# Hybrid trunk: output projection as seven block products, longer attention turns, and the first tile's norm weights applied by column

## The chip, the cores and the metric

The kernel runs on one core of a Trainium2 chip. The metric is the device time of one execution in microseconds (us); lower is better. The median of three runs of the kernel before is 843.53 us (843.45 to 843.87). Five engines work side by side, each through its own queue in order: PE (TensorE, matrix products and transposes), DVE (VectorE), ACT (ScalarE), POOL (GpSimd) and SP, whose queue issues nearly all DMAs here. Products are collected in PSUM, operands lie in SBUF, and some intermediate tensors go through DRAM.

## What is computed

One layer on a 1024 x 1024 float32 input (S = D = 1024):

```python
h    = rmsnorm(x, norm_pre)
proj = h @ w_in                      # split by columns
oa   = rmsnorm(diff_attention(qa, ka, va, lam), norm_a) * (1 - lam_init)   # 4 heads, causal, ALiBi
ya   = oa * silu(za)
hb   = rmsnorm(sigmoid(ob) * mlstm(silu(conv(qb)), silu(conv(kb)), vb, ig, fg), norm_b)   # 4 heads
yb   = hb * silu(zb)
merged = sigmoid(ga) * (ya @ w_a) + sigmoid(gb) * (yb @ w_b)
out  = x + rmsnorm(merged @ w_out, norm_post)
```

## The kernel before

Every large product is done with operands cut in two parts, high and low (`split`, L113 to L115: ACT casts the high part, DVE subtracts it for the low part), and three products per block of 128: high x high, high x low, low x high. So a full 128 x 128 x 512 step is three matmuls.

**Opening (L162 to L232, L247, L604 to L627).** `x` comes in eight tiles of 128 tokens. Eight warm-up matmuls on a tile of ones (L168, L169) run first on PE, then two matmuls of one row (L174) spread the row `norm_pre` over 128 partitions, and ACT copies the two halves from PSUM to `npre` (L175). `norm_tile` (L206) squares and sums a tile (L211, L215), takes the power -0.5 on POOL (L221), and multiplies the tile by that factor and by `npre` in one DVE instruction (L223). `turn_tile` (L233) turns the tile by eight PE transposes (L83) and splits the result. `tok_pass` (L292) multiplies it with the first 520 weight columns, in two chunks whose raw parts are `raw_c` and whose split parts are `wc`.

**Seven-product blocks (L316 to L437).** The other projections go by pairs of 128 columns. A pair is a 2 x 2 block product, done with seven products in place of eight (`PRODS`, Winograd's form of Strassen's method). `Combos` forms sums of the blocks of `w_in` on DVE, `Banks` forms the sums of the results: three PSUM banks Y, X, Z, into which products are added, and three copies out (`keep`). One product is 12 matmuls of 512 columns (`product`, L367). The operand of product n+2 is prepared (`prep`) while n runs.

**Weaving (L1011 to L1050).** Products of the projections, and later `merge_b`, are a list of generators, `fill`. Through `weave` the mLSTM and attention chains take from it: after each step of the chain, `weave` emits fill worth a wanted number of us (a step of six matmuls is counted as 1.4), with a debt `left` carried over and at least 0.6 of the wanted share. `attn_head` (L924) does a head in ten turns. Turn i emits `weigh(i-2)` (`pv`), `turn(i-1)` (`pT`), `score(i, 0)` and `score(i, 1)` (`S`, then a DVE reduction L949 and an ACT exponential L956), and `combine(i)` (L965, L966, L970), then yields its share. The transposes `pT` of the next turn need the result of L970. Before the output stage PE's order is pinned to that of the program; the other engines' orders are set by a scheduler.

**The end (L1109 to L1232).** `merge` multiplies `yb` and then `ya` with their weights; each unit (8 x 2 of them) is 12 matmuls, a DVE instruction that applies the gate (L1108) and, for `ya`, the addition of the other branch (L1181) and a split into `M`. The output projection then walks two column halves of `w_out`, eight token tiles each: 24 matmuls into one bank, sum of squares on ACT (L1209), product with `norm_post` on DVE (L1213). In the second half each row is finished: POOL (L1220, L1221), two DVE instructions with `x` (L1226), two stores (L1230).

## Time and profile before

| what | us |
|---|---|
| median of the three runs | 843.53 |
| the profiled execution's own time | 841.9 |
| its span, first to last instruction | 840.2 |
| PE busy | 829.3 (99%) |
| DVE busy | 573.0 (68%) |
| ACT busy | 400.4 (48%) |
| `ya` merge on PE starts | 691.8 |
| output projection on PE starts | 746.3 |

All times below are counted from the span's start. Busy times are unions of intervals. A row such as "2.72 PE ob0Y L80 x12" is twelve matmuls that took 2.72 us together. A bracket at the end of a row, [0.69 <-ACT m L114], is the idle time of the engine before that instruction and what ended it. Names are those of the program's tiles without buffer numbers; a name before the arrow is written, those behind are read. The matmuls' ends are modelled and overlap, so the spacing of starts says more than a single duration.

### The profile page before, as it was taken

The numbers are of one execution on the slowest core, as the hardware profiler recorded it, in microseconds if no ns is written. First come the engines' busy times: TensorE is split into PE (matmuls) and PEld (weight loads), VectorE is DVE, ScalarE is ACT, GpSimd is POOL, SyncE is SP. The second block draws the span as 40 slices with busy tenths as digits, with TensorE's granted clock in tenths as the row PEclk, the third lists the DMA queues.
The fourth block names the chain that finished last, engine by engine and source line by source line (L and its number), as shares of the span: only waits on it lengthen the run. The fifth ranks groups of instructions, "written<-read, shape, count | busy, mean of one in ns | idle before, by whom it ended". The sixth has DMA issues, their size and how long they took to land.

```text
span 840.2 us, 12224 instructions
## 1 busy us (share of the span) xinstructions
PE 829.3 (99%) x4282; PEld 706.5 (84%) x4282; DVE 573.0 (68%) x1161; ACT 400.4 (48%) x892; POOL 36.5 (4%) x70
## 2 busy tenths in 40 slices
PE   9999999999999999999999999999999999999997
PEld 7998888888888888888888888788888888888885
DVE  6996969769659767568767875587587734981133
ACT  6663545444544544446655655466576521341110
POOL 1100000000000000010010000000100000000011
PEclk9999999999999999999999999999999999999999
DMA  7712441451542547266256426442666757830252
GB/s 238 216 40 70 101 151 51 138 163 51 176 143 83 174 146 231 89 208 202 92 161 228 126 74 204 139 162 75 224 208 229 271 184 263 295 105 1 101 200 101
DMA packets 100482, 128.44 MB, mean 153 GB/s; under 512 B 8666, under 2 KB 60098, under 8 KB 100420
## 3 DMA queue, kind: packets, MB, share of 16 engines
q1 hardware_dynamic: 100420, 127.66, 47.9%
q8 instruction: 34, 0.56, 0.3%
q14 instruction: 28, 0.23, 0.1%
HBM read 88.27 MB, written 39.35 MB: 152 GB/s over the span
## 4 chain that ended last, share of the span: by engine, by line
PE 95%; DMA 2%; DVE 1%; ACT 1%; issue 1%; SPq 0%; POOL 0%; DVEq 0%; POOLq 0%; ACTq 0%
PE out L80 10%; PE mrg L80 10%; PE tok L80 6%; PE S L80 4%; PE pv L80 4%; PE pT L83 2%; PE num L80 2%; PE qkb0Y L80 1%; PE g04Y L80 1%; PE g00Y L80 1%; PE za1Y L80 1%; PE g12Y L80 1%; PE g02Y L80 1%; PE zb0Y L80 1%; PE za0Y L80 1%; PE g10Y L80 1%
## 5 line engine op out<-in xcount | busy, mean ns | idle before, releaser
L956 ACT ACTIVATE p<-p,ast 128x128 f32<-128x128 f32 (+7 forms) x64 | 49.5, 775 | 31.2 <-DVE ast L955 23.5
L949 DVE CUSTOM_DVE_ANT_0 p<-S,gm 128x384 f32<-128x384 f32 (+5 forms) x96 | 49.8, 554 | 13.4 <-PE S L80 11.7
L1213 DVE TENSOR_TENSOR o<-out,npost 128x512 f32<-128x512 f32 x16 | 11.1, 691 | 57.3 <-ACT oj L1209 57.3
L80 PE MATMUL mrg<-y,mbw 128*128 128x512 f32 x192 | 44.9, 391 | 0.0
L80 PE MATMUL mrg<-y,maw 128*128 128x512 f32 x192 | 43.7, 389 | 0.0
L1209 ACT ACTIVATE oj<-out 128x512 f32<-128x512 f32 x16 | 9.6, 598 | 71.5 <-PE out L80 71.5
L80 PEld LDWEIGHTS mrg<-y,maw 128*128 128x128 f32 x192 | 36.0, 188 | 7.5
L80 PEld LDWEIGHTS mrg<-y,mbw 128*128 128x128 f32 x192 | 35.8, 188 | 7.3
L80 PEld LDWEIGHTS pv<-va,pT 128*128 128x128 f32 x288 | 37.2, 191 | 2.6
L80 PE MATMUL pv<-va,pT 128*128 128x128 f32 x288 | 37.4, 275 | 0.0
L80 PE MATMUL S<-khh,qs 128*128 128x384 f32 (+5 forms) x96 | 34.9, 369 | 0.3 <-ACT pT L986 0.2
L80 PE MATMUL S<-kll,qs 128*128 128x384 f32 (+5 forms) x96 | 32.4, 342 | 0.4 <-DMA kll<-qk_d 0.4
L1108 DVE SCALAR_TENSOR_TENSOR tg<-tg,mrg 128x512 f32<-128x512 f32 x32 | 21.8, 682 | 14.6 <-PE mrg L80 12.9
L754 DVE SCALAR_TENSOR_TENSOR cv<-pad,cols,cv 128x1024 f32<-128x1024 f32 x24 | 30.7, 1280 | 0.2
L970 DVE SCALAR_TENSOR_TENSOR p<-p,ast,p 128x128 f32<-128x128 f32 (+7 forms) x32 | 26.1, 816 | 0.7
L823 ACT ACTIVATE junk<-raw 128x128 bf16<-128x128 f32 x32 | 9.9, 310 | 31.6 <-DVE raw L818 31.4
L80 PE MATMUL out<-wo,m 128*128 128x512 f32 x96 | 23.7, 395 | 0.0
L83 PE MATMUL pT<-ident,p 128*128 128x128 f32 x144 | 21.2, 274 | 2.5 <-DVE p L970 2.5
L986 ACT COPY pT<-pT 128x512 f32<-128x512 f32 (+3 forms) x48 | 21.9, 488 | 2.7 <-PE pT L83 2.5
L80 PEld LDWEIGHTS out<-wo,m 128*128 128x128 f32 x96 | 18.0, 188 | 4.4 <-DVE m L115 0.2
L995 ACT ACTIVATE oa<-pv 128x128 f32<-128x128 f32 x32 | 8.8, 276 | 26.3 <-PE pv L80 26.1
L80 PE MATMUL out<-wot4h,m 128*128 128x512 f32 x64 | 21.1, 390 | 0.0
(1240 smaller groups left out, 2465.4 us busy)
## 6 DMA issues: line engine op xcount, KB each, us to landing
raw_g<-in_w_in_dram SPq DMA_DIRECT2D x16, 512.0 KB, 3.6
g_d<-g SPq DMA_DIRECT2D x32, 256.0 KB, 3.6
tg<-g_d SPq DMA_DIRECT2D x32, 256.0 KB, 3.5
raw_qkb<-in_w_in_dram SPq DMA_DIRECT2D x16, 256.0 KB, 3.2
z_d<-zt SPq DMA_DIRECT2D x16, 256.0 KB, 2.8
zs<-z_d SPq DMA_DIRECT2D x16, 256.0 KB, 4.6
raw_qka<-in_w_in_dram SPq DMA_DIRECT2D x16, 256.0 KB, 3.1
qk_d<-qah SPq DMA_DIRECT2D x16, 256.0 KB, 2.3
```

Of the source, the lines that this page charges most:

```text
L80: pin(nc.tensor.matmul(*args, **kw))
L83: pin(nc.tensor.transpose(out=out, in_=in_, identity=ident))
L754: nc.vector.scalar_tensor_tensor(out=cv, in0=pad[:, t : t + S], scalar=cols[:, t * 8 + blk : t * 8 + blk + 1], in1=cv, op0=ALU.mult, op1=A ...
L823: nc.scalar.activation(junk, raw[:, c, 0:P], AF.Square, accum_out=stbs[h, c // 4][:, 1, c % 4 : c % 4 + 1])
L949: nc.vector.tensor_tensor_reduce(out=pr[:, n0:n1], in0=pss[:, : n1 - n0], in1=gm[:, (7 - i) * P + n0 : (7 - i) * P + n1], scale=-0.125, sc ...
L956: nc.scalar.activation(pr[:, :nk], pr[:, :nk], AF.Exp, bias=nm, scale=-1.0, accum_out=sth[:, c, i : i + 1],)
L970: nc.vector.scalar_tensor_tensor(out=p0[:, :nk], in0=p1[:, :nk], scalar=st[:, 3:4], in1=p0[:, :nk], op0=ALU.mult, op1=ALU.add,)
L986: nc.scalar.copy(pT[:, j0:j1], pt[:, 0 : (j1 - j0) * P].rearrange("p (j t) -> p j t", t=P))
L995: nc.scalar.activation(raw[:, i], pv[:, 0:P], AF.Square, accum_out=sth[:, 2, i : i + 1])
L1108: nc.vector.scalar_tensor_tensor(out=tg, in0=tg, scalar=1.0, in1=ps, op0=ALU.add, op1=ALU.mult)
L1209: nc.scalar.activation(junk, ps, AF.Square, scale=D ** -0.5, accum_out=ssq[:, tt, cc : cc + 1])
L1213: nc.vector.tensor_mul(orr[:, c0 : c0 + 512], ps, npost[:, c0 : c0 + 512])
```

## The change

Three things are changed.

**Output projection.** The 1024 x 1024 product becomes four pairs of token tiles (p and p+4), each done with the seven products of `PRODS`; now the moving operands are seven combinations of blocks of `w_out` (`WO`), and the stationary ones are combinations of blocks of `M`. `M` stays unsplit float32, and `finish_a` only adds. The weights are loaded and combined in five steps per half while the `ya` merge runs (`wo_first`, `wo_both`); the last two (`22`, `t4`) are split in the first pair. The early split of two `w_out` blocks in `merge_b` is gone. Results go through `Banks` and `out_sink`; a row is finished when both its halves are there.

**Attention turns.** `weave` gets a lower bound: a turn takes at least min(its share, 5.2 us) of fill, whatever the debt, and 2.5 us are pulled before the first head.

**Opening.** Twelve warm-up matmuls in place of eight. The first tile is only scaled by its own factor (one half on DVE, one on ACT); `norm_pre` is loaded a second time as 8 x 128, turned by PE into a column per block (`npcol`), and applied by DVE when the turned tile leaves PSUM (`turn_first`). The row is spread over the partitions by the two one-row matmuls behind the first tile's transposes. ACT's and DVE's orders are pinned up to the end of the second chunk's split (`hold`).

```diff
-WARM = 8
+WARM = 12
+CHAIN = 5.2
...
-    npre = slot(12, [P, D], "npre")
-    for n0 in range(0, D, 512):
-        prow, pn = temp("prow")[0:1, :], misc("npre")
-        nc.sync.dma_start(prow, norm_pre[:, n0 : n0 + 512])
-        nc.tensor.matmul(pn, ones[0:1, :], prow, start=True, stop=True)
-        nc.scalar.copy(npre[:, n0 : n0 + 512], pn)
+    warm(WARM)
+    pcol = temp("pcol")[0:8, 0:P]
+    nc.sync.dma_start(pcol, norm_pre[0].rearrange("(b p) -> b p", p=P))
+    pc8 = misc("npcol")
+    tr(out=pc8[:, 0:8], in_=pcol, identity=ident[0:8, 0:8])
...
+        if tt == 0:
+            hold(nc.vector.tensor_scalar(xt[:, 0:512], xt[:, 0:512], st[:, 2:3], None, ALU.mult))
+            hold(nc.vector.tensor_copy(npcol.rearrange("p k a -> p (k a)"), pc8[:, 0:8]))
+            hold(nc.scalar.activation(xt[:, 512:], xt[:, 512:], AF.Copy, scale=st[:, 2:3]))
...
+    def turn_first():
+        xt = x_tiles[0]
...
+        high(raw0[0], chunk0[0][0])
+        for half, block in enumerate(first[0]):
+            pt = misc(f"xT_0_{half}")
+            for i in range(4):
+                turn128(
...
+            hold(nc.vector.tensor_mul(
+                v4(block), v4(pt), npcol[:, half * 4 : half * 4 + 4].to_broadcast([P, 4, P])
+            ))
+            high(v4(block), his[half])
+        spread = []
+        for half in range(2):
+            spread.append(misc("npre"))
+            tc.keep_in_program_order(nc.tensor.matmul(
+                spread[half], ones[0:1, :], prow[half], start=True, stop=True
+            ))
+        low(v4(first[0][0]), his[0], los[0])
+        for half in range(2):
+            hold(nc.scalar.copy(npre[:, half * 512 : half * 512 + 512], spread[half]))
...
-    def weave(chain):
+    def weave(chain, least=0.0):
...
-            now = max(due, 0.6 * want)
+            now = max(due, 0.6 * want, min(want, least))
...
+    def wo_first(g):
+        b11, b12, b22, b21 = (
+            wo_load(kh, cc, g, home)
+            for kh, cc, home in ((0, 0, 10), (0, 1, 11), (1, 1, 12), (1, 0, 8 + g))
+        )
+        yield
+        wo_split("11", g, b11)
+        yield
+        nc.vector.tensor_sub(b12, b12, b11)
+        wo_split("t1", g, b12)
+        yield
+        nc.vector.tensor_sub(b22, b22, b12)
+        wo_split("t2", g, b22)
+        yield
+        nc.vector.tensor_sub(b11, b22, b11)
+        wo_split("t3", g, b11)
+        yield
+        wo_split("21", g, b21)
+        yield
+        nc.vector.tensor_sub(b21, b21, b22)
+        t4_raw.append(b21)
...
-        weave(attn_head(h, stk, gm, supply, before if h else None, after, res))
+        weave(attn_head(h, stk, gm, supply, before if h else None, after, res), CHAIN)
...
-        nc.vector.tensor_add(tg, tg, mb)
-        split(tg, M[d // 4, half, 0][:, d % 4], M[d // 4, half, 1][:, d % 4])
+        nc.vector.tensor_add(M[d // 4, half][:, d % 4], tg, mb)
...
-        for tt in range(NT):
...
-            for kt in range(KT):
-                for i, (a, b) in enumerate(((0, 0), (0, 1), (1, 0))):
-                    mm(
-                        ps, M[kt // 4, tt // 4, a][:, kt % 4, js], wide[cc, kt // 4, kt % 4, b],
-                        start=(kt == 0 and i == 0), stop=(kt == KT - 1 and i == 2),
-                    )
...
+            orr, src = orow[tt], bank
+            if kept is not None:
+                src = orr[:, ns]
+                nc.vector.tensor_add(src, kept, bank)
...
+            nc.vector.tensor_mul(orr[:, ns], src, npost[:, ns])
...
+        def prep(self, i):
+            t = wc_tile([P, 2, 4, P], f"ow{self.p}{i}")
+            self.ops[i] = t
+            if i == 2:
+                self.cb.early()
+            self.cb.make(PRODS[i][0], t[:, 0], t[:, 1])
...
+    for n, (p, i) in enumerate(steps):
+        if n + 2 < len(steps):
+            q, i2 = steps[n + 2]
+            outs[q].prep(i2)
...
+        if n in (0, 1):
+            wo_split("22", n, wo_load(1, 1, n))
+        if n in (2, 3):
+            wo_split("t4", n - 2, t4_raw[n - 2])
+        outs[p].run(i)
```

The change moves instructions on PE and DVE. On PE at the very start, before: `xT` are the transposes of the first tile (its two halves), `tok` the first products with `h11h`, the turned tile's high part.

```order
L169 MATMUL warm<-ones 128x128 x8
L174 MATMUL npre<-prow,ones 128x512 x2
L83 MATMUL xT_0_189<-ident,x_99 128x128 x4
L83 MATMUL xT_1_196<-ident,x_99 128x128 x4
L80 MATMUL tok<-wc_181,h11h 128x264 x4
```

And now, at the same place on PE:

```order
L184 MATMUL warm<-ones 128x128 x12
L87 MATMUL npcol<-ident,pcol 128x8
L84 MATMUL xT_0_189<-ident,x_99 128x128 x4
L84 MATMUL xT_1_196<-ident,x_99 128x128 x4
L283 MATMUL npre<-prow,ones 128x512 x2
L81 MATMUL tok<-wc_178,h11h 128x264 x4
```

The two one-row matmuls moved from ahead of the transposes to between them and the first product.

On PE in the third head's first turn, before: `S` are the scores, `qka3Z` and the like are fill, `pT` the transposes that wait for the turn's DVE chain.

```order
L80 MATMUL S<-kll_2_5258,qs_2_5254 128x128
L80 MATMUL qka3Y<-ht2h,qka3w_5315 128x512
...
L80 MATMUL qka3Y<-ht2h,qka3w_5315 128x512
L80 MATMUL qka3Z<-ht1h,qka3w_5361 128x512
...
L80 MATMUL qka3Z<-ht1h,qka3w_5361 128x512
L83 MATMUL pT<-ident,p_5415 128x128
```

And now, at the same turn on PE:

```order
L81 MATMUL S<-kll_2_5267,qs_2_5263 128x128
L81 MATMUL qka3Z<-ht1h,qka3w_5370 128x512
...
L81 MATMUL qka3Z<-ht1h,qka3w_5370 128x512
L81 MATMUL qka3Y<-ht3h,qka3w_5406 128x512
...
L81 MATMUL qka3Y<-ht3h,qka3w_5406 128x512
L84 MATMUL pT<-ident,p_5443 128x128
```

Between scores and transposes stood 6 + 6 matmuls, and now stand 6 + 12. In the next two turns of this head it was 13 and 19 matmuls, and is 24 each. In the last turns (scores of blocks 5 to 7) it was 35 or 36 in several heads, and is 24 in all four, but for those turns in which an earlier deadline pulls more.

On DVE around the end of the `ya` merge, before: `tg<-tg,mrg` is a unit's gate, `tg<-tg,mb` the addition, `m` the split of `M`, `wot2l`, `wot1l` low parts of `w_out`, `o<-out,npost` the first rows of the output stage.

```order
L1108 SCALAR_TENSOR_TENSOR tg<-tg,mrg 128x512
L115 TENSOR_TENSOR m_6966<-tg,m_6965 128x512
L1181 TENSOR_TENSOR tg<-tg,mb 128x512
L115 TENSOR_TENSOR wot2l<-raw_o_7598,wot2h 128x1024
L115 TENSOR_TENSOR m_6968<-tg,m_6967 128x512
L115 TENSOR_TENSOR wot1l<-raw_o_7604,wot1h 128x1024
L115 TENSOR_TENSOR wot1l<-raw_o_7608,wot1h 128x1024
L1213 TENSOR_TENSOR o_7339<-out,npost 128x512
```

And now on DVE, from the gate of the last unit on: `ow` are the low parts of the stationary operands of the first pair's products (here those of the second and the third product), `os` a combination of blocks of `M`, `wo22l` and `wot4l` the low parts of the two late combinations of `w_out`.

```order
L1201 SCALAR_TENSOR_TENSOR tg<-tg,mrg 128x512
L124 TENSOR_TENSOR ow_7368<-m_6962,ow_7368 128x512
L1270 TENSOR_TENSOR m_6963<-tg,mb 128x512
L124 TENSOR_TENSOR wo22l<-raw_o_7403,wo22h 128x1024
L388 TENSOR_TENSOR os_0_7361<-m_6963,m_6961 128x512
L124 TENSOR_TENSOR wot4l<-o_7023,wot4h 128x1024
L124 TENSOR_TENSOR ow_7371<-os_0_7361,ow_7371 128x512
```

Between the last unit of the merge and the operand of the third product now stand five DVE instructions (the last merge addition and two low parts of weights among them), where the first output rows before needed the splits of `M` alone.

More of the change, by code (lines that the diff above doesn't have):

```diff
@@ L612 @@
             load_x(n + 3)
+        if n == 0:
+            for raw, (hi, lo) in zip(raw1, chunk1):
+                split(raw, hi, lo)
+            opening[0] = False
         if n + 2 < NT:
             norm_tile(XO[n + 2])
-        if n == 0:
-            chunk1 = split_chunk(1, raw1)
         nxt_rest = turn_tile(XO[n + 1]) if n + 1 < NT else None
@@ new lines, in wo_home, with wo_slots, wo_split @@
+    def wo_home(name, tags):
+        two = [hp.tile([P, 4, 512], F32R, tag=f"h{t}", name=f"wo{name}{e}") for t, e in zip(tags, "hl")]
+        WO[name] = [[two[e][:, g * 2 : g * 2 + 2] for g in range(2)] for e in range(2)]
+    def wo_slots(name, first_):
+        WO[name] = [
+            [slot(first_ + e * 2 + g, [P, 2, 512], f"wo{name}{e}{g}", F32R) for g in range(2)]
+            for e in range(2)
+        ]
+    def wo_split(name, g, raw):
+        split(raw, WO[name][0][g], WO[name][1][g])
@@ L1076, in load_y, with wo_both @@
+    def wo_both():
+        yield from wo_first(0)
+        yield from wo_first(1)
     def load_y(slot0, heads, tags):
@@ new lines, in finish_row @@
+    def finish_row(tt):
+        ts_ = slice(tt * P, (tt + 1) * P)
+        orr = orow[tt]
+        st = sp.tile([P, 3], F32, tag="ost", name="ost")
+        nc.gpsimd.tensor_add(st[:, 0:1], ssq[:, tt, 0:1], ssq[:, tt, 1:2])
+        nc.gpsimd.tensor_tensor(st[:, 2:3], st[:, 0:1], mhalf[:, 0:1], ALU.pow)
+        xr = raw_tile([P, D], f"xr{tt}")
+        nc.sync.dma_start(xr, x[0, ts_, :])
+        for n0 in range(0, D, 512):
+            ns = slice(n0, n0 + 512)
+            nc.vector.scalar_tensor_tensor(
+                out=orr[:, ns], in0=orr[:, ns], scalar=st[:, 2:3], in1=xr[:, ns],
+                op0=ALU.mult, op1=ALU.add,
+            )
+            nc.sync.dma_start(out[0, ts_, ns], orr[:, ns])
```

184 lines of the change are left out of this document (110 added, 74 removed).

## Prediction

> **What bounds the kernel now.** I read the page's first lines, then the chain that ended last, then PE's own waits.
>
> ```profile
> span 840.2 us, 12224 instructions
> PE 829.3 (99%) x4282; PEld 706.5 (84%) x4282; DVE 573.0 (68%) x1161; ACT 400.4 (48%) x892; POOL 36.5 (4%) x70
> PE 95%; DMA 2%; DVE 1%; ACT 1%; issue 1%; SPq 0%; POOL 0%; DVEq 0%; POOLq 0%; ACTq 0%
> ```
>
> PE is busy for 99% of the span and holds 95% of the chain. So time goes away in two ways only: fewer matmuls, or fewer holes between them. The pieces of the chain give the price of a matmul:
>
> ```profile
> 84.17 2.72 PE ob0Y L80 x12
> 746.25 87.83 PE out L80 x384
> ```
>
> Twelve matmuls of 512 columns, one product of a projection, take 2.72 us, 0.2267 us each. The last stage's 384 matmuls at that price are 87.0 us; it took 87.83, so it has no holes worth naming. The holes that PE saw are few, says the view of its waits (total, times, longest):
>
> ```profile
> PE pT L83 <- DVE p L970: 2.5, 2, 1.5
> ```
>
> 2.5 us in attention behind the softmax chain is by far the largest sum in that view. The opening hardly shows in it: its loss is slow work, as shown below.
>
> **Output projection: the removed work.** Before: 384 matmuls, which is 32 times twelve. After: four pairs of seven products, 28 times twelve, 336. Four products less at 2.72 us: **-10.9 us**, on the path, since that stage is PE back to back. This holds as long as the other engines feed the products. What they now do:
>
> ```profile
> L1213 DVE TENSOR_TENSOR o<-out,npost 128x512 f32<-128x512 f32 x16 | 11.1, 691 | 57.3 <-ACT oj L1209 57.3
> L1226 DVE SCALAR_TENSOR_TENSOR o<-o,ost,xr 128x512 f32<-128x512 f32 x16 | 11.3, 748 | 1.8 <-POOL ost L1221 1.8
> ```
>
> Per pair DVE has 4 sums of blocks, 7 low parts, 3 additions of kept results, 4 products with the norm's weights and 4 row endings: 22 instructions of about 0.69 us, 15.2 us, against 7 x 2.72 = 19.0 us of PE. ACT has 7 high parts, 3 copies and 4 squares, 14 at about 0.6 us, 8.4 us. Both fit, with 80% and 44%. It is more than it seems that is free on DVE, since instructions start closer than they last:
>
> ```profile
> 11.39 0.68 DVE L115 TENSOR_TENSOR h11l<-xT,h11h 128x512 fp32r<-128x512 f32 x1
> 11.99 1.25 DVE L115 TENSOR_TENSOR wc<-raw_c,wc 128x1056 fp32r<-128x1056 f32 x1
> 13.16 0.68 DVE L115 TENSOR_TENSOR h21l<-xT,h21h 128x512 fp32r<-128x512 f32 x1
> ```
>
> 0.60 us from start to start for 512 columns and 1.17 us for about 1024. An operand is prepared two products (5.4 us) ahead, so a row's ending that waits in DVE's queue for ACT and POOL stops no product as long as it waits less than that. In steady state I cost the new work at nothing; the cover is PE's 2.72 us per product, and without it each DVE instruction would cost its 0.6.
>
> **Merge and boundary: the added wait.** During the `ya` merge (15 intervals of 2.72 us, 40.8 us) DVE by the new order has 41 instructions of 512 columns and 12 of 1024: 41 x 0.60 + 12 x 1.17 = 38.6 us, 95% of it. Before, it had slack there and still ran late:
>
> ```profile
> 746.85 0.69 DVE L115 TENSOR_TENSOR m<-tg,m 128x512 fp32r<-128x512 f32 x1 [0.69 <-ACT m L114]
> 749.92 0.68 DVE L1108 SCALAR_TENSOR_TENSOR tg<-tg,mrg 128x512 f32<-128x512 f32 x1
> ```
>
> The last unit's gate began at 749.92, 3.7 us after its last matmul (746.25). That cost nothing, because the first output tiles need only the first token half of `M`. Now the third product needs a combination of all four blocks, so the last unit. With DVE on time, its operand is ready after the gate, `ow`, the addition, `wo22l`, `os`, `wot4l` and `ow`: 0.26 + 5 x 0.60 + 2 x 1.17 = 5.6 us; the third product starts 5.4 us after the merge and reads the low part at its third matmul, 0.45 us on. So punctual DVE costs nothing and each us of lateness costs about one. Bounds: 0, and 5 us (the old 3.7 and one more 1024 pass). I take **+1.5 us**, below the middle, since the chain gate, addition, ACT cast, split (which set the old lateness) is gone. From there 71 to 80% of load lets DVE catch up.
>
> **Tail.** The last matmul is followed by square, product, POOL, two row instructions, store. That chain stays; the other row of the last pair now ends only one product (2.7 us) ahead of it:
>
> ```profile
> 834.17 0.60 ACT L1209 ACTIVATE oj<-out 128x512 f32<-128x512 f32 x1 [4.75 <-PE out L80]
> 835.79 1.41 DVE L1226 SCALAR_TENSOR_TENSOR o<-o,ost,xr 128x512 f32<-128x512 f32 x2 [0.21 <-POOL ost L1221]
> ```
>
> From square to row ending it takes 1.62 us, the ending 1.41. The earlier row's square starts 2.72 - 0.6 (its addition) = 2.1 us ahead, so it is done 0.9 us into the last chain; its pair of stores goes ahead of the last. **+0.2 us**, at most 0.6.
>
> **Attention turns.** The two holes in PE:
>
> ```profile
> 544.10 0.39 PE L80 MATMUL qka3Z<-ht1h,qka3w 128*128 128x512 f32 x1
> 545.94 0.30 PE L83 MATMUL pT<-ident,p 128*128 128x128 f32 x1 [1.45 <-DVE p L970]
> 550.35 0.47 PE L80 MATMUL qka3Y<-ht3h,qka3w 128*128 128x512 f32 x1
> 551.85 0.44 PE L83 MATMUL pT<-ident,p 128*128 128x128 f32 x2 [1.02 <-DVE p L970]
> ```
>
> By starts less one matmul: 545.94 - 544.10 - 0.23 = 1.6 and 1.3 us, together 2.9. These turns had 12 and 13 matmuls of fill; 18 and 24 stand there now, 1.4 and 2.5 us more. Both go. The DMA wait at the first head:
>
> ```profile
> 376.13 0.28 PE L80 MATMUL S<-khh,qs 128*128 128x128 f32 x1
> 376.81 0.30 PE L80 MATMUL S<-kll,qs 128*128 128x128 f32 x1 [0.41 <-DMA kll<-qk_d]
> ```
>
> 0.68 - 0.11 = 0.6 us, and the 2.5 us pulled ahead cover it. What pays: the last turns of the heads shrink from 36 to 24 fill matmuls, 8.2 to 5.4 us. The longest turn of the first head shows whether that is enough:
>
> ```profile
> 423.07 0.39 PE L80 MATMUL S<-kll,qs 128*128 128x512 f32 x1
> 428.74 1.28 DVE L970 SCALAR_TENSOR_TENSOR p<-p,ast,p 128x1024 f32<-128x1024 f32 x1
> 431.49 1.73 PE L80 MATMUL pv<-va,pT 128*128 128x128 f32 x14
> 433.05 1.04 PE L83 MATMUL pT<-ident,p 128*128 128x128 f32 x8
> ```
>
> From the last score to the end of L970: 428.74 + 1.28 - 423.07 = 6.95 us. With 24 matmuls PE has 0.23 + 5.44 + 1.56 (the `pv` group, 433.05 - 431.49) = 7.2 us before `pT`. Just enough here. In the fourth head's turn 6 the chain took more:
>
> ```profile
> 650.50 0.36 PE L80 MATMUL S<-kll,qs 128*128 128x448 f32 x1
> 657.28 1.15 DVE L970 SCALAR_TENSOR_TENSOR p<-p,ast,p 128x896 f32<-128x896 f32 x1
> 658.92 1.50 PE L80 MATMUL pv<-va,pT 128*128 128x128 f32 x12
> 660.26 0.93 PE L83 MATMUL pT<-ident,p 128*128 128x128 f32 x7
> ```
>
> 657.28 + 1.15 - 650.50 = 7.9 us against 0.2 + 5.44 + 1.34 = 7.0: up to 0.9 us of new hole if DVE is as loaded as then. I take 0.5 in all: -2.9 - 0.6 + 0.5 = **-3.0 us**. Bounds -4.5 (smaller holes go too) and -1 (0.6 us in each of four late turns).
>
> **Opening.**
>
> ```profile
> 1.10 3.78 PE L169 MATMUL warm<-ones 128*128 128x128 f32 x16 [1.10 <-DVE mprev L699]
> 4.81 3.78 PE L174 MATMUL npre<-prow,ones 1*128 1x512 f32 x4
> 10.82 1.23 PE L80 MATMUL tok<-wc,h11h 128*128 128x264 f32 x4
> 12.13 1.25 PE L80 MATMUL tok<-wc,h11l 128*128 128x264 f32 x4
> 14.93 1.08 PE L80 MATMUL tok<-wc,h21l 128*128 128x264 f32 x4
> 15.81 0.83 PE L80 MATMUL tok<-wc,h21h 128*128 128x264 f32 x4
> 20.18 1.62 PE L80 MATMUL tok<-wc,b 128*128 128x264 f32 x12
> ```
>
> Sixteen warm-up records in 3.78 us, about 0.22 each (the `pv` records above, as large, take 1.56 / 14 = 0.11), then the one-row matmuls at about 0.9: PE runs at half speed. `tok` does too: (15.81 - 14.93) / 4 = 0.22 us a matmul, and 1.62 us for twelve at 20.18. The group at 15.81 is the first that is shorter, so full speed comes about 16.2. The first product waits behind the spread of the norm weights:
>
> ```profile
> 5.35 0.56 POOL L221 TENSOR_TENSOR xst<-xst,mhalf 128x1 f32<-128x1 f32 x1 [3.35 <-DVE xst L220]
> 7.60 0.75 DVE L223 SCALAR_TENSOR_TENSOR x<-x,xst,npre 128x512 f32<-128x512 f32 x1 [2.34 <-ACT npre L175]
> 14.57 1.28 DVE L223 SCALAR_TENSOR_TENSOR x<-x,xst,npre 128x1024 f32<-128x1024 f32 x1 [0.67 <-POOL xst L221]
> 18.21 0.69 DVE L115 TENSOR_TENSOR b<-xT,b 128x512 fp32r<-128x512 f32 x1
> ```
>
> The factor is there at 5.9, but DVE waits 2.3 us for `npre`. Now the first tile is scaled at once (about 5.8, one small DVE instruction less), turned at about 6.6 behind 24 warm-up records, and multiplied by the columns. But the four one-row records then stand ahead of `tok`. At half speed they last 3.4 us and `tok` starts near 12.0; at full speed 1.7 us, near 9.3. The case turns on whether 24 records (1.1 to 6.4 us, 5.3 us) bring PE to full speed; before, 16 records (3.4 us) did not, and 4.1 us of `tok` from 12.13 did. I take it that they do. Behind it ACT and DVE bind. From 9.3 ACT has two copies, a cast of 1056 columns and the square of the second tile, 2 x 0.6 + 2 x 1.1 = 3.4 us (0.60 for 512 columns at 834.17, near twice that for 1024): 12.7, with the factor 13.7. There L223 starts, before at 14.57; with two low parts of weights behind it, 13.7 + 3 x 1.17 = 17.2, the second tile's low part, before at 18.21. So its products could start near 18 and not at 20.18. But DVE's queue is full there with the next tiles' parts; I take about half, **-1.2 us**, with bounds -2.3 and +0.3 (a further DMA issue and the longer warm-up).
>
> The Trainium skill (TensorE: Matmul & The Clock Gate, Part 1) says that the clock is released after one busy window of about 3.4 us, that the windows run free of the program, and (Part 4) that transposes do not count as busy. The trace agrees where it can: 3.4 us of warm-up did not release the clock, 4.1 us of `tok` did. By that rule a stretch of 5.3 us holds a whole window in (5.3 - 3.4) / 3.4, some 55%, of the phases (an estimate from that page), and the sum is 830.1 in those and 831.3 in the others.
>
> **The sum.** -10.9 + 1.5 + 0.2 - 3.0 - 1.2 = -13.4 us. The profiled execution took 841.9 us, its span and 1.7 us around it; by the sum 828.5. The median of the runs shown, 843.5, lies 1.6 above; the same difference gives **830.1 us**.
>
> **Rivals.**
>
> *Slow clock at the opening.* The 24 records do not release the clock; `tok` starts near 12.0 and the opening gives nothing: 831.3. For it: the one-row matmuls and transposes between did not keep PE fast before; against: 5.3 us is longer than the 4.1 that did it.
>
> *DVE late at the boundary.* At 95% load, one late DMA in the merge is not made up, as in the gate at 749.92; +5 in place of +1.5: 833.6.
>
> *The holes move to the last turns.* At 24 matmuls, turns 6 and 7 wait 0.6 to 0.9 us in most heads: about 3 us more than I count, 833.
>
> *DVE binds the output stage, slower than before.* DVE takes its instructions in order, and each row's ending waits for ACT and POOL 1.6 us; each low part can wait 0.69 for its ACT cast, as at 746.85. If all were real, a pair would last 15.2 + 2 x 1.6 + 7 x 0.69 = 23.2 us in place of 19.0: +16.8 over four pairs, 847. It decides once a pair takes over 19.0 + 13.4 / 4 = 22.4 us. Against it: the waits overlap with other instructions in the new order, and spacing is 0.60. If half is real, 21.1 us a pair, the gain shrinks to 5 us: 838.5.
>
> **Chances.** Forecast 0.48 (830.1, its own range 828 to 832.5), slow clock 0.22, late boundary 0.14, late turns 0.08, half-bound output 0.04, slower 0.04. The range that leaves out no more than 2 in 10 is 826.3 (the good bounds are -10.9 - 4.5 - 2.3 = -17.7, 825.8; not quite all of them at once) to 835.0 (a late boundary with a slow clock, 833.6 + 1.2). A measurement of this kernel can tell about 0.2%, 1.7 us, from no change: faster by more than that 0.95, within it 0.01, slower 0.04.
>
> **What would show it.** Right: 336 `out` matmuls in about 76 us without PE waits behind `ow`; the `pT` wait of 2.5 us gone; `tok` starts near 9.3 at 0.12 us spacing. Wrong: PE idle in the third product of the first pair (boundary), PE waiting at `pT` in turns 6 and 7, one-row records at 0.85 us, or a gap before each product of the later pairs (DVE bound).

## The result, and the profile after

The changed kernel takes 829.67 us (median of 4 runs, 829.21 to 832.56), the kernel before 843.49 us measured beside it: ratio 0.9858, 95% interval 0.9843 to 0.9873. In the next series of runs it took 831.75 us against 842.24 us (0.9871, 0.9852 to 0.9890). It is 10.5 to 13.8 us faster; the forecast was 830.1 us, from 826.3 to 835.0. The execution profiled first is the slowest of its four, 832.56 us, and that matters below.

The page's first lines and the chain by engine:

```profile
span 830.8 us, 12245 instructions
PE 817.2 (98%) x4243; PEld 696.6 (84%) x4243; DVE 613.4 (74%) x1216; ACT 420.7 (51%) x921; POOL 45.4 (5%) x70
PE 86%; DMA 5%; DVE 4%; issue 2%; SPq 1%; ACT 1%; POOL 0%; DVEq 0%; POOLq 0%
```

PE's share of the chain fell from 95% to 86%; DMA and DVE now hold 9% of it. PE's waits (total, times, longest) say where:

```profile
PE mrg L81 <- DVE maw L124: 2.2, 1, 2.2
PE mrg L81 <- DVE tg L1201: 1.7, 2, 1.1
PE qka1Z L81 <- ACT qka_p L414: 1.0, 1, 1.0
```

The 2.5 us behind `p` at `pT` are gone. In their place PE waits in the two merges for DVE, 3.9 us, and once in attention for ACT. The pieces of the chain around the start of the output projection (start, us, what):

```profile
739.93 7.28 PE mrg L81 x32
747.21 2.72 PE out0Y L81 x12
749.93 2.72 PE out0X L81 x12
752.65 2.79 PE out0Y L81 x12
```

One product starts when the one before it ends, the third too, where the forecast had put the wait. From the start of the first to the start of the last matmul of the output projection it is 76.70 us, before 87.59.

The opening by PE's timeline:

```profile
1.10 4.68 PE L184 MATMUL warm<-ones 128*128 128x128 f32 x24 [1.10 <-DVE mprev L763]
7.56 1.98 PE L283 MATMUL npre<-prow,ones 1*128 1x512 f32 x4
9.46 0.75 PE L81 MATMUL tok<-wc,h11h 128*128 128x264 f32 x4
17.74 1.62 PE L81 MATMUL tok<-wc,b 128*128 128x264 f32 x12
```

The four one-row records take 1.98 us in place of 3.78, `tok` starts at 9.46 in place of 10.82, the second tile at 17.74 in place of 20.18.

**Where the first profile lost time.** In the second merge DVE waits for a raw block of the output weights:

```profile
714.98 0.68 DVE L1270 TENSOR_TENSOR m<-tg,mb 128x512 f32<-128x512 f32 x1
718.95 1.23 DVE L1150 TENSOR_TENSOR o<-o,o 128x1024 f32<-128x1024 f32 x1 [3.29 <-DMA o<-in_w_out_dram]
```

From there to the boundary DVE's instructions stand without a gap, and it is still late 13 us on, when PE needs the low part of the next block of `w_a`:

```profile
728.67 4.01 PE L81 MATMUL mrg<-y,maw 128*128 128x512 f32 x17
734.85 6.46 PE L81 MATMUL mrg<-y,maw 128*128 128x512 f32 x20 [2.16 <-DVE maw L124]
```

That hole is followed by something that the forecast did not have. The stretches of 2 us (start:end and length, then busy time with counts of PE, PEld, DVE, ACT and POOL, then the granted clock, DMA's busy share and GB/s):

```profile
734.00:736.00 2.00, 1.15 (x4) 0.93 (x5) 2.00 (x5) 0.00 (x0) 0.00 (x0) 0.81 0.62 202
736.00:738.00 2.00, 2.00 (x6) 1.62 (x5) 2.00 (x3) 0.00 (x0) 0.00 (x0) 0.50 0.69 225
738.00:740.00 2.00, 2.00 (x9) 1.54 (x9) 2.00 (x4) 0.00 (x0) 0.00 (x0) 0.84 0.65 212
```

From 736 to 738 PE is busy all the time, and gets 6 matmuls done where 9 or 10 are usual: the clock is at 0.50 for about 3.4 us (2 us at 0.50, and 0.81 and 0.84 are what 0.8 and 0.6 us of it make of a stretch), eight matmuls start 0.43 us apart instead of 0.23, and that costs another 1.55 us. By the distance of starts, PE loses 2.3 us in the first merge's end, 2.3 at this hole and 1.6 at half clock: 6.2 of the 6.4 us that it loses between attention and the output projection. The first of the three has other loads behind it than the block above: in the first merge DVE waits 3.29 and 2.40 us for two raw blocks of the first group, and PE then waits for the gates (`tg`); the second execution, below, has 0.84 and 0.68 us there and no such hole. (The `ya` merge is counted here from its first matmul with `w_a`, at 699.43 us; in the profile of before that is 702.57. The 691.8 us given above for before is still the merge of `yb`.)

### The profile page after: what moved, and what is told of

It is laid out like the page before. It is cut to its first block, busy times and chain, and to the rows that moved or that the text cites. A ratio compares the mean times of both kernels' runs of the same rounds, so it can differ in the third digit from the quotient of the medians.

```text
span 830.8 us, 12245 instructions
## 1 busy us (share of the span) xinstructions
PE 817.2 (98%) x4243; PEld 696.6 (84%) x4243; DVE 613.4 (74%) x1216; ACT 420.7 (51%) x921; POOL 45.4 (5%) x70
## 4 chain that ended last, share of the span: by engine, by line
PE 86%; DMA 5%; DVE 4%; issue 2%; SPq 1%; ACT 1%; POOL 0%; DVEq 0%; POOLq 0%
PE tok L81 5%; PE S L81 4%; PE mrg L81 4%; PE pv L81 3%; PE pT L84 2%; PE num L81 2%; PE qkb0Y L81 1%; PE out0Y L81 1%; PE za1Y L81 1%; PE g04Y L81 1%; PE g12Y L81 1%; PE g06Y L81 1%; PE g00Y L81 1%; PE g14Y L81 1%; PE qkb1Y L81 1%
## 5 line engine op out<-in xcount | busy, mean ns | idle before, releaser
L1013 DVE CUSTOM_DVE_ANT_0 p<-S,gm 128x384 f32<-128x384 f32 (+5 forms) x96 | 49.7, 554 | 13.8 <-PE S L81 11.6
L81 PE MATMUL mrg<-y,maw 128*128 128x512 f32 x192 | 45.6, 400 | 2.2 <-DVE maw L124 2.2
L81 PEld LDWEIGHTS mrg<-y,maw 128*128 128x128 f32 x192 | 37.1, 194 | 10.5 <-DVE maw L124 2.6
L124 DVE TENSOR_TENSOR ow<-m,ow 128x512 fp32r<-128x512 f32 x24 | 16.4, 688 | 10.2 <-ACT ow L121 10.1
L121 ACT CAST ow<-m 128x512 fp32r<-128x512 f32 x24 | 14.8, 621 | 17.0 <-DVE m L393 1.7
L642 DVE SCALAR_TENSOR_TENSOR y<-yT,cols,zs 128x512 f32<-128x512 f32 x16 | 12.0, 748 | 10.3 <-DMA zs<-z_d 7.1
L81 PEld LDWEIGHTS S<-khh,qs 128*128 128x128 f32 x96 | 18.1, 188 | 1.8 <-ACT pT L1050 0.4
L604 ACT ACTIVATE g<-g 128x512 f32<-128x512 f32 x24 | 15.1, 630 | 8.0 <-DVE g L603 5.6
```

The lines of the kernel that those rows point to most:

```text
L81: pin(nc.tensor.matmul(*args, **kw))
L121: hold(nc.scalar.copy(hi, raw))
L124: hold(nc.vector.tensor_sub(lo, raw, hi.bitcast(F32)))
L604: nc.scalar.activation(st, bank if kept is None else st, AF.Tanh, scale=0.5)
L642: nc.vector.scalar_tensor_tensor(out=y, in0=pt, scalar=ncol, in1=zs, op0=ALU.mult, op1=ALU.mult)
L1013: nc.vector.tensor_tensor_reduce(out=pr[:, n0:n1], in0=pss[:, : n1 - n0], in1=gm[:, (7 - i) * P + n0 : (7 - i) * P + n1], scale=-0.125, sc ...
```

## The experiments

Two theories stood at the start. *The terms*: the gain is the four products (-10.9), the closed holes in attention (-3.0) and the opening (-1.2); what is lost in the merge comes from one DMA that lands late, which a DVE at 95% load cannot make up. Its rivals: the turns and the opening only move the time elsewhere, and the merge is lost because DVE is full in any case. After the first run there were three series (in the table four rows, then four, then four), each with the kernel before beside its variants; a ratio is to the kernel before of its own series.

| run | median us (range) | ratio to before, 95% interval | profiled: `ya` merge / output, us |
|---|---|---|---|
| first run of the change | 829.67 (829.21 to 832.56) | 0.9858, 0.9843 to 0.9873 | 47.61 / 76.70 |
| same, series 1 | 831.75 (829.54 to 832.33) | 0.9871, 0.9852 to 0.9890 | 43.95 / 78.30 |
| old turns | 833.85 (833.02 to 834.73) | 0.9901, 0.9884 to 0.9919 | 44.24 / 80.07 |
| 16 warm-up records | 834.60 (832.40 to 835.76) | 0.9904, 0.9886 to 0.9921 | 48.14 / 76.77 |
| other homes | 828.02 (826.65 to 831.49) | 0.9839, 0.9819 to 0.9860 | 43.52 / 77.83 |
| opening of before, series 2 | 830.69 (829.58 to 832.43) | 0.9867, 0.9846 to 0.9887 | 43.61 / 78.33 |
| other homes, POOL's queue | 833.49 (832.41 to 835.73) | 0.9904, 0.9883 to 0.9924 | 47.83 / 80.72 |
| +1 DVE instruction a product | 831.00 (830.35 to 832.53) | 0.9870, 0.9848 to 0.9893 | 48.00 / 76.97 |
| +2 a product | 845.52 (842.55 to 848.01) | 1.0040, 1.0016 to 1.0064 | 43.66 / 93.25 |
| other homes, series 3 | 827.42 (826.84 to 828.84) | 0.9825, 0.9794 to 0.9856 | 43.52 / 77.93 |
| same, additions on POOL | 833.07 (832.39 to 835.71) | 0.9904, 0.9871 to 0.9936 | 43.52 / 79.85 |
| output part alone | 836.74 (833.41 to 837.36) | 0.9924, 0.9897 to 0.9952 | 44.05 / 80.03 |
| POOL additions, opening of before | 835.69 (833.27 to 839.02) | 0.9922, 0.9892 to 0.9952 | 45.03 / 83.75 |

The last column is worked out from the traces: from the first matmul of the second merge to the first of the output projection (43.52 without a hole, and in the profile of before), and from there to the last (76.70 without one).

### The change once more

> The changed kernel once more, in one call with its variants and the kernel before. If the forecast's sum is right the ratio to before is 0.984 to 0.987 again (829 to 832 us). Both theories of the merge (a late DVE behind one late load; a DVE that is too full) expect a sum of PE's holes of 3 to 7 us in the merge; they differ in the run with the other homes.

Same source, another execution. Its PE waits:

```profile
PE tok L81 <- ACT wc L121: 1.1, 2, 0.9
PE pT L84 <- DVE p L1034: 0.8, 1, 0.8
PE qka1Z L81 <- ACT qka_p L414: 0.7, 1, 0.7
PE out0Y L81 <- ACT ow L121: 0.4, 1, 0.4
PE out0Y L81 <- DVE ow L124: 0.3, 1, 0.3
```

No wait in the merge, no half clock there; the wait now stands at the third product, behind `ow`, where the forecast had it. The output stage is 78.30 us, 1.6 more than in the first profile, the merge 0.4 over its least: 2.0 us against 6.4, and less than the 3 to 7 us that both theories had expected. The wait for the raw block is here all the same, and no shorter:

```profile
715.97 1.23 DVE L1150 TENSOR_TENSOR o<-o,o 128x1024 f32<-128x1024 f32 x1 [3.56 <-DMA o<-in_w_out_dram]
```

So the length of that wait does not decide what it costs. What differs is when it ends: 17.5 us after the merge's first matmul here, 19.5 in the first profile, where the loads ahead of it had already made DVE late (waits of 3.29, 2.40 and 3.46 us, here 0.84, 0.68 and 1.16). In all eight profiles with the block's old home and the merge's additions on DVE it comes out so: ended at 15.8 to 17.5 us (five profiles) no hole over 0.6 us in the `ya` merge, at 19.5 to 20.1 (three) a hole of 2.3 to 2.9 us. The lateness has two forms, then. Either DVE misses a weight block inside the merge, and PE pays the hole and the half clock; or it just makes it, and the lateness reaches the boundary, where it costs 1.6 us here and 3.3 and 3.4 in two others. The spans of the two profiled executions, 830.8 and 827.8 us, differ by 3.0, most of the range of the change's eight runs.

### The old attention turns

```
-    pull(2.5)
-        weave(attn_head(...), CHAIN)
+        weave(attn_head(...))
```

> The changed kernel with the attention turns of before (no lower bound per turn, nothing pulled ahead of the first head). Theory, that the longer turns closed the two holes at pT and the one at kll and cost little at the heads' ends: slower than the changed kernel by 3.0 us (2.5 to 3.5), about 832.7, with PE waits of 2.5 us at pT back. Rival, that the fill moved out of the last turns is paid there and the holes only move: slower by under 1 us.

```profile
PE pT L84 <- DVE p L1034: 2.5, 2, 1.5
PE S L81 <- DMA kll<-qk_d: 0.5, 1, 0.5
```

All three holes come back, and it is 2.1 us slower by the medians of the series (833.85 - 831.75), 2.5 by the ratios. The two intervals touch, so the time alone would not rule out the rival's 1 us; the holes in the profile do. By the distance of starts, PE loses 7.4 us between 360 and 680 us here, 7.3 before; with the new turns 4.2 in the first profile, 5.1 in the second and 3.5 with the other homes. The theory holds, at two thirds to nearly all of its size. Part of the gain is given back in two places. One is the hole at `qka1Z`, 0.6 to 2.0 us in nine of eleven profiles with the new turns: with work pulled forward, the product comes before ACT, which had waited for a DMA (2.5 us for `raw_za` in the first profile), has kept the bank that it needs. The other is the fourth head's turn 6, 0.6 to 1.1 us in five of them and 2.3 in one.

### 16 warm-up records in place of 24

```
-WARM = 12
+WARM = 8
```

> The changed kernel with 16 warm-up records in place of 24. Theory, that the long warm-up is what brings PE to full speed before the products: the four one-row records take 3.4 us in place of 2.0, the first product starts 1 us or more later, the second tile 1 to 2.3 us later, and the kernel is 1.0 to 2.3 us slower (831 to 832). Rival, that the norm weights by column alone give the opening's gain, since the products behind it run into full speed anyway: within 0.5 us of the changed kernel.

```profile
1.10 3.47 PE L184 MATMUL warm<-ones 128*128 128x128 f32 x16 [1.10 <-DVE mprev L763]
7.44 3.74 PE L283 MATMUL npre<-prow,ones 1*128 1x512 f32 x4
11.11 1.25 PE L81 MATMUL tok<-wc,h11h 128*128 128x264 f32 x4
19.28 1.61 PE L81 MATMUL tok<-wc,b 128*128 128x264 f32 x12
```

As the theory had it, the one-row records run at half speed, and `tok` starts 1.7 us and the second tile 1.5 us later than in the first profile. But 16 records are not too short to reach full speed: the last two start 0.15 and 0.11 us apart, where those before were 0.21 apart. PE then idles ahead of the transposes, and the clock falls just as the one-row records begin (at 7.5 us by these rows):

```profile
6.42 1.09 PE L84 MATMUL xT<-ident,x 128*128 128x128 f32 x8 [1.70 <-DVE x L249]
6.00:8.00 2.00, 1.58 (x9) 1.32 (x10) 1.32 (x4) 1.28 (x2) 0.00 (x0) 0.88 1.07 307
8.00:10.00 2.00, 2.00 (x3) 0.66 (x2) 1.47 (x3) 1.91 (x4) 0.00 (x0) 0.50 1.02 362
```

In the first profile that idle time is 0.60 us. So the eight further records also close a pause, and which of the two keeps the clock up (the longer work or the shorter pause) no run here separates. The time is 2.85 us longer in the same series, more than the opening explains; in the profile the rest stands in the merge, with half clock behind it:

```profile
PE mrg L81 <- DVE maw L124: 2.8, 1, 2.8
```

### The opening of before

The changed kernel with all parts of the diff but those of the opening.

> The changed kernel with the whole opening of before (norm weights spread by TensorE first, 16 warm-up records, old order); output projection and turns as changed. Theory, that the opening is worth the 2.3 us by which the first unit of the mLSTM's projections starts earlier in the profiles (65.87 to 63.59 us): slower than the changed kernel by 1.7 to 2.3 us, and first products of the second tile at 20.2. With 16 warm-up records alone the second tile started at 19.28, 1.0 ahead of before; so the columns would be worth about 0.9 to 1.0 us of it and the warm-up about 1.3. Rival, that the columns are worth nothing without the long warm-up: the same time as with 16 warm-up records (834.6), within 0.5 us.

Both expectations failed: 0.9867 lies between the change's two ratios, where 1.7 to 2.3 us more or the 834.6 us of the run with 16 records were expected. The profile says why:

```profile
1.10 3.64 PE L170 MATMUL warm<-ones 128*128 128x128 f32 x16 [1.10 <-DVE mprev L702]
4.67 1.98 PE L175 MATMUL npre<-prow,ones 1*128 1x512 f32 x4
8.88 1.23 PE L81 MATMUL tok<-wc,h11h 128*128 128x264 f32 x4
18.42 1.62 PE L81 MATMUL tok<-wc,b 128*128 128x264 f32 x12
```

The same code as before, the same 16 records, and this time the one-row records run at full speed; the second tile starts 1.76 us earlier than in the profile of before. The half clock comes behind them, from 7.9 to 14.7 us, as these stretches show:

```profile
6.00:8.00 2.00, 1.30 (x6) 0.42 (x4) 1.45 (x2) 1.73 (x3) 0.00 (x0) 0.97 1.06 300
8.00:10.00 2.00, 1.89 (x8) 1.69 (x8) 1.77 (x3) 1.16 (x3) 0.00 (x0) 0.50 1.00 370
14.00:16.00 2.00, 2.00 (x17) 2.00 (x17) 2.00 (x3) 1.20 (x3) 0.00 (x0) 0.83 0.82 309
```

So one profile of a kernel does not give the price of its opening. Over all profiles: with the old opening (before and three runs here) the second tile started at 20.18, 18.42, 18.56 and 19.40 us, mean 19.14; with the new one and 24 records, nine profiles, at 17.74 to 18.29, mean 17.91. The difference is 1.23 us, and the nine lie close together. In all nine the one-row records took 1.98 us; with the old opening they took 1.98, 1.98, 2.10 and 3.78. Full speed does not last in all nine: in five of them the clock is at 0.50 again for 3.4 us, from between 9.5 and 10.7 us on, and `tok` runs at half speed there. The second tile starts no later for it (17.79 to 18.14, against 17.74 to 18.29 in the other four), so PE does not set its start; the forecast had ACT and DVE bind there. The Trainium skill (TensorE: Matmul & The Clock Gate, Part 1) says that the clock's windows run free of the program and that the same kernel meets them in another phase from run to run; the four executions of the old opening agree.

### Another home for one raw block

```
-  for kh, cc, home in ((0, 0, 10), (0, 1, 11), (1, 1, 12), (1, 0, 8 + g))
+  for kh, cc, home in ((0, 0, 10 - g), (0, 1, 11), (1, 1, 12), (1, 0, 8 + 2 * g))
-  orow[tt] = slot((10, 11, 12, 8)[len(orow) % 4], ...)
+  orow[tt] = slot((9, 11, 12, 8)[len(orow) % 4], ...)
```

> The changed kernel with another place for one raw block of the output weights: the second group's b11 goes to slot 9, which is free early, and its b21, used last, to slot 10. Theory, that DVE is late in the second merge because it waits 3.3 us for this one load: that wait goes, with it PE's hole of 2.2 us behind the low part maw and the 1.6 us at half clock behind the hole; 2 to 4 us faster than the changed kernel in the profiled span, 1 to 4 in the median. Rival, that DVE's load of 95% itself binds the merge: the wait at the load goes, but PE's holes of 2 us and more stay and the time is within 0.7 us.

> The run with b11 of the second group in slot 9, once more beside its variants. If its gain was the removed wait: 826.5 to 829 us again, no PE hole of 2 us in the second merge. If the first time was luck: as the changed kernel, 829.7 to 832.

The second group's b11 no longer waits for slot 10. In the second run with it, DVE:

```profile
687.35 1.22 DVE L1150 TENSOR_TENSOR o<-o,o 128x1024 f32<-128x1024 f32 x1
713.40 0.69 DVE L1270 TENSOR_TENSOR m<-tg,mb 128x512 f32<-128x512 f32 x1
715.77 1.23 DVE L1153 TENSOR_TENSOR o<-o,o 128x1024 f32<-128x1024 f32 x1 [1.69 <-DMA o<-in_w_out_dram]
```

and PE:

```profile
PE qka1Z L81 <- ACT qka_p L414: 0.8, 1, 0.8
PE out0Y L81 <- ACT ow L121: 0.4, 1, 0.4
PE out0Y L81 <- DVE ow L124: 0.3, 1, 0.3
```

L1150 runs 30 us earlier and without a wait; half of the wait shows again at the next load (1.69 us). Both profiles have the second merge at 43.52 us, without any hole, and keep 1.1 to 1.2 us at the boundary. The first merge still loses 1.3 us in one of them. The theory holds: 3.7 us faster than the change in the same series by the medians, 2.7 by the ratios (whose intervals just overlap), and 827.42 us in series 3. With 0.9825 and 0.9839 it is the fastest version here.

### The loads of the output weights from POOL's queue

This run has the other homes too.

```
-        nc.sync.dma_start(r, w_out_v[...])
+        nc.gpsimd.dma_start(r, w_out_v[...])
```

> The run with the other homes (b11 to slot 9), and the loads of the output weights issued by POOL in place of SP. Theory, that the loads come late because they stand in SP's queue behind loads of tg that wait for buffers: DVE's waits for o in the first group (2.9 and 1.8 us in the run with the other homes) fall below 1 us, PE's hole of 1.2 us behind the gates near 687 goes, and it is 1 to 2 us faster than that run, about 826.5. Rival, that slots or the transfers themselves set the landing: the waits stay and the time is within 0.7 us of 828.

It went the other way, 5.5 us slower than the other homes alone. DVE's waits late in attention and in the merge:

```profile
DVE y L642 <- DMA zs<-z_d: 7.6, 1, 7.6
DVE o L1153 <- DMA o<-in_w_out_dram: 3.6, 2, 3.3
DVE o L1150 <- DMA o<-in_w_out_dram: 2.6, 1, 2.6
```

The median time from issue to landing of the eight early loads is 6.0 us from POOL's queue, and 6.6 and 6.0 us in the two profiles with the other homes from SP's. The first wait in the first group stayed (2.61 us, against 2.91), the second fell from 1.81 to 0.30: a place behind others in SP's queue is not the main thing that sets the landing. What is new is that `zs` lands late: DVE waits 7.6 us for it, where the run with SP's queue waited 1.9. `y` is late, PE waits 1.9 us for it in the merge, half clock follows. Why `zs` is late was not settled.

### How much of DVE's time in the output stage is free

```
+        for _ in range(1):   # 2 in the second
+            t = ...operand prepared last...
+            nc.vector.tensor_mul(part("dummy"), t[:, 0]..., npost[:, 0:512])
```

> The changed kernel with one more DVE instruction of 512 columns per product of the output projection (28 in all; its result is not used, nothing is left out). Theory, that the forecast's cover holds: 22 x 0.60 = 13.2 us of work per pair against 19.0 of PE, so seven more (17.4 us) cost nothing, or under 1.5 us in all at the first pair, where DVE is late. Rival, that DVE's waits for ACT and POOL already use up the slack and DVE nearly binds: about 4.2 us per pair, 8 to 15 us in all, about 840 or more.

> The same with two more DVE instructions per product (56 in all). Theory: 22 x 0.60 + 14 x 0.60 = 21.6 us per pair against 19.0: DVE binds, 2.6 us per pair, 8 to 11 us in all, about 840, with PE waits behind the operands' low parts in every pair. Rival, that the waits come on top: 2 x 4.2 us per pair, 25 us or more in all, about 855.

One more instruction per product costs nothing (831.00 us; the output stage 76.97 against 76.70). A stretch of 19 us in the middle pairs, of the change:

```profile
768.00:787.00 19.00, 19.00 (x85) 15.59 (x84) 13.54 (x22) 8.56 (x18) 3.48 (x6) 1.00 0.32 110
```

and with one more:

```profile
768.00:787.00 19.00, 19.00 (x84) 15.59 (x84) 17.50 (x28) 8.43 (x18) 5.42 (x6) 1.00 0.31 107
```

22 instructions in 13.5 us, as worked out from the spacing (22 x 0.60 = 13.2). At 17.5 of 19.0 us PE is still never idle. With two, DVE binds: the middle pairs take 21.0 and 23.5 us by their first matmuls, against 21.6 worked out, and the kernel is 14 us slower than the change. The excess over the worked-out 8 to 11 us is again partly the clock: the holes of 1.75 and 0.53 us close together at 768 to 770, and of 1.97 us at 815, are each followed by 1.4 to 1.6 us lost at half speed. The tail is 2.6 us longer.

### DVE's load in the merge, relieved by POOL

With the other homes, and

```
-        nc.vector.tensor_add(M[d // 4, half][:, d % 4], tg, mb)
+        add = (nc.gpsimd if d < 6 else nc.vector).tensor_add
+        add(M[d // 4, half][:, d % 4], tg, mb)
```

> The same with 12 of the 16 additions m<-tg,mb of the second merge on POOL in place of DVE (12 x 0.60 = 7.2 us of DVE's 38.6 us). Theory, that DVE's load of 95% is why nothing late is made up: DVE reaches the boundary on time, the holes there (about 1.8 us with the other homes) shrink below 0.5 us, and it is 1.0 to 2.0 us faster than the run with the other homes. Rival, that the boundary's holes come from the chain of preparation itself (gate, operand, sum, low parts) and not from lateness: within 0.7 us of it.

5.6 us slower than the other homes alone; the gain that the theory forecast did not come, nor the rival's equal time. POOL's additions as a group, and three of DVE's instructions:

```profile
L1271 POOL TENSOR_TENSOR m<-tg,mb 128x512 f32<-128x512 f32 x12 | 20.7, 1744 | 33.4 <-DVE tg L1201 28.7 <-DMA mb<-m_d 4.6
```

```profile
709.32 2.31 DVE L1161 TENSOR_TENSOR o<-o,o 128x1024 f32<-128x1024 f32 x1
711.55 1.21 DVE L124 TENSOR_TENSOR wo11l<-o,wo11h 128x1024 fp32r<-128x1024 f32 x1
744.82 0.69 DVE L1201 SCALAR_TENSOR_TENSOR tg<-tg,mrg 128x512 f32<-128x512 f32 x1 [1.94 <-DMA tg<-g_d]
```

An addition takes 1.74 us on POOL and 0.69 on DVE; while POOL works, some of DVE's instructions last twice as long (2.31 against 1.21); and at the merge's end DVE waits 1.94 us for a load of `tg`, likely since POOL holds the buffer longer (not tested). The Trainium skill (SBUF — State Buffer, section "SBUF: two separate sides") says that a DVE instruction with two SBUF inputs and a POOL instruction that reads SBUF exclude each other for a whole instruction; the doubled durations agree. The boundary's holes grew from 1.23 to 3.15 us. Some 2.6 of the 5.2 us by which its profile is longer lie elsewhere, at `qka1Z` with half clock behind it, where the edit changes nothing. DVE did get time in the merge: busy 36.9 of 44 us, against 41.3 with its additions. But the new wait stands at the end, where nothing makes it up, so whether a less loaded DVE alone would close the boundary's holes stays open.

### The output part alone, and the opening once more

The first has before's opening and turns, the second is the run above with before's opening.

> The kernel before with the new output projection and its merge alone (opening and attention turns of before). By the terms: -10.9 for four products, +0.6 for the tail as the changed kernel's profile shows it, +2 to +4 for holes in merge and boundary: 6.3 to 8.3 us faster than before, 834 to 836. Rival, that the boundary's lateness comes only through the new turns and the earlier end of the attention stage: 10 us faster, 832.

> The run with additions on POOL and other homes, with the whole opening of before. With the merge's holes taken out, the difference of the two is the opening's worth alone. Theory, that the phase of the clock's windows decides it: the opening of before is at full speed for the one-row records in some executions (the first product at 8.9 us) and not in others (10.8), so its median is 0.8 to 1.7 us slower. Rival A: 2.3 us slower, the difference of the first two profiles. Rival B: no difference, within 0.5 us.

The output part alone gives 5.5 us by the medians, 6.4 by the ratio, at the low end of the worked-out 6.3 to 8.3 and with an interval (4.0 to 8.7) that holds them; the rival's 10 is out. In its profile the boundary costs 3.3 us. With the run of the old turns (output and opening, 0.9901) and the change (0.9858 and 0.9871) the parts are, by ratios: 6.4 for the output, 1.9 for the opening, 2.5 to 3.6 for the turns. The opening by pairs of runs: 1.9 us here, 1.5 (2.6 by medians) with the additions on POOL, and for the opening of before against the change between 0.8 slower and 0.3 faster. With intervals of about 2 us on each, time alone shows no more than that it is near 1; the profiles' 1.2 us is the better figure, and the last run does not tell its theory (0.8 to 1.7) from its rival A (2.3). Its profile also has a hole of 3.3 us at the boundary, with the clock at 0.50 for 6.8 us behind it: DVE waits 2.68 us for a load of `tg` at the merge's end, as in the run above (1.94), so its time holds more than the opening.

## Why the prediction was right, step by step

| term | forecast | first profile | second profile |
|---|---|---|---|
| output projection | -10.9 | -10.9 | -10.9 |
| merge and boundary | +1.5 (0 to 5) | +6.4 | +2.0 |
| tail | +0.2 | +0.6 | +0.6 |
| attention turns | -3.0 | -3.1 | -2.2 |
| opening | -1.2 | -2.3 | -1.7 |
| sum | -13.4 | -9.3 | -12.2 |

Against the 840.2 us span of before, the spans changed by -9.4 and -12.4 us. The first profile's 6.4 us include the 2.3 us at the end of the first merge. The second profile's output term is its 78.30 us without the 1.6 us of holes, which stand in the row below.

That the first median lies 0.4 us from the forecast is in part luck. The next series has the gain at 10.5 us, not 13.8. In both profiles the merge cost more than its term, by 4.9 and 0.5 us, and the opening gave more, by 1.1 and 0.5, in the main because the profile of before had a late second tile (20.18 us, mean of four 19.14).

- *What bounds it.* PE's matmuls and holes; it stayed so. Four products less gave exactly their price wherever the boundary was fed.
- *DVE in the output stage* at nothing: right. The cover is worth 4 us per pair, which one run used up without loss and the next overran.
- *Merge and boundary*: the mechanism was right in kind, late loads that a full DVE does not make up, and so was the place in the second profile. The first has it at two other places, inside the `ya` merge and, behind two other loads, at the end of the first merge, for which the forecast had no term; inside the `ya` merge the step "each us of lateness costs about one" failed, since a hole of 2.3 us cost 3.9. The bound of 5 us was too low for that case (6.4). The rival that named a late DVE priced it at +5 at the boundary, and had a chance of 0.14; in six profiles (the change twice, 16 records, old opening, old turns, one more DVE instruction) the lateness cost 6.4, 2.0, 6.1, 1.7, 4.6 and 4.8 us, so in four of six it was nearer the rival's size than the forecast's, and the chance was too low.
- *Tail*: mis-sized by 0.4 us. The earlier row's ending on DVE (1.42 us from 824.34) waited for POOL and ends at 825.7, so the last product with the norm's weights starts 0.8 us later behind the last matmul's square than before.
- *Attention turns*: right in size. The 0.5 us allowed for new holes covered the fourth head's turn 6 in most profiles; the hole at `qka1Z` was not foreseen.
- *Opening*: the case on which it turned came out as taken: behind 24 records the one-row records run at full speed, in nine profiles of nine, where the prediction's estimate had 55% of the phases. Its premise, that 16 records do not bring PE to full speed, was read from one profile and is wrong in general: in four of five profiles with 16 they did, and the clock fell again at 7.4 to 8.5 us. Its 3.4 us for 16 records, and for the one-row records at half speed, are 3.7 by the starts in the rows that it shows. The term is -1.2 over many profiles, as forecast. The profile of before showed an unlucky phase of its own opening, which a single profile could not tell.
- *The rivals.* The slow clock did not come for the one-row records; the late turns showed in one profile (2.3 us); DVE binding the output stage needs 14 more instructions per pair.

## What to carry to other kernels

Where an engine is nearly full beside the bottleneck (DVE 41.3 of 44 us in the merge), look at every DMA that it waits for in that stage, and at what frees the buffer that the DMA writes: one block moved to a buffer that was free earlier, so that its first use ran 30 us sooner, was worth about 3 us here, while the runs with work moved to an idle engine or loads to an idle queue were 5 to 6 us slower, each with a new DMA wait of DVE. A short stage at the start has to be judged over several profiles, since the clock meets it in another phase each time. And a removed product gives its full price only if the stage in front of it hands over in time.

## What the runs showed of the hardware

- **A hole of about 2 us or more in PE's work costs 1.2 to 1.6 us more.** In fourteen profiles, behind the opening, holes of 1.97, 2.32, 2.33, 2.74, 2.93 and 3.33 us, and pairs of holes that add up to 2.3 to 2.5 us within 3 us, were each followed by about 3.4 us at half speed (6.8 us behind the longest, with 2.5 us lost); single holes up to 1.6 us, and pairs up to 1.8, were not. The Trainium skill (TensorE: Matmul & The Clock Gate, section "Why this matters for your kernels") asks for no gaps over about 3 us; these rows show the loss from about 2 us, and the measurement decides.
- **The granted clock in the opening is not all there is.** In the profile of before its column reads 1.00 while four one-row records take 3.78 us; the durations tell the speed there.
- **Full speed can be given and taken back within the opening.** In nine of the thirteen profiles of changed kernels the clock is back at 0.50 from between 7.4 and 10.7 us on, for 3.4 us with 24 warm-up records and 6.8 with 16.
- **POOL beside DVE**: an addition of 512 columns 1.74 us against 0.69, and some of DVE's own instructions of 1024 columns 2.31 us against 1.21 while POOL works.
